# Projections in feature-major form with 512 tokens a matmul, and block-diagonal rotary queries for the sample, in a two-layer streaming encoder

## The chip, the cores and the metric

The kernel runs on one core of one Trainium2 chip. The metric is the device time of one execution in microseconds (us). A measurement of this kernel's time is good to some tenths of a per cent.

## The reference

Two layers of an encoder run over two groups of inputs with the same weights: a prompt of 1,024 tokens (one sequence) and a sample of 8 sequences of 16 tokens each, which continue caches of 512 earlier frames. Width is 1,024. In each layer one projection of x gives everything else:

```python
h = jnp.einsum('btd,de->bte', x, w_in)
(c_q, c_kv, k_rope, g_mla, f_q, f_k, f_v, f_logit, g_fox, m_q, g_mem) = jnp.split(h, split_idx, axis=-1)
```

Three kinds of attention follow, four heads each. MLA: queries and keys from low-rank latents (`c_q` of 384, `c_kv` of 256), with a part of 128 and a rotary part of 64 per head; a query sees keys up to its chunk of 64. Forgetting attention ("fox"): heads of 64, causal, with a bias of summed log forget values. Memory attention: heads of 64 over 256 memory rows. Each output is multiplied by `silu` of its gate (`g_mla`, `g_fox`, `g_mem`), all go through `w_out`, and `y = LayerNorm(alpha * x + out)`. For the sample the MLA score of a query against a cached frame is the product of latents (256) plus the product of rotary parts (64). Outputs are both y and the new cache rows. Everything is float32.

## The kernel before

**Precision.** Most matmuls take split operands: a value is a high part (`fp32r`) plus a low part, and `mm3` (L189) adds three products per pair: high by high, high by low, low by high (lines L193 to L195 of the profile). `split` (L173) makes the parts: a copy on ACT, a subtraction on DVE. `wsplit` (L183) does it for weights, with the subtraction on DVE or POOL. The sample's attention uses plain float32 operands (`mm`, L197).

**x^T.** A layer's input lies transposed in SBUF: feature on the partition, token along the row. Before, `X` has four entries, one per 256 tokens, each of two halves of four feature chunks (tiles of 128 x 4 x 256, high and low); a fifth entry is the sample. `xtok` (L253) cuts 128 tokens of one chunk out of it. In the first layer `xload` in `main` (L1462) loads x^T ready-made from DRAM in pieces of 512 KB and splits it; in the second `xpair` (L224) transposes two finished output tiles on TensorE and splits them. The first two pairs are made in the tail of the first layer, the last two are read back from DRAM after it (`after0`, L1494).

**Two forms of projection.** `tokproj` (L284) has tokens on the output's partitions: 128 tokens of x^T are the stationary operand, the weights move (up to 306 columns). `featproj` (L287) is feature-major: 128 weight columns are stationary, one entry of x^T moves, 256 tokens, into half a PSUM bank; 8 chunks x 3 products = 24 matmuls a group. It is used by `gates` (L356: memory gate `ge`, fox gate `gf`, two MLA gates `gm0`, `gm1`, each 2 x 4 groups and one token-major group for the sample) and by `qproj` (L343: memory queries, 2 x 4 groups, and fox queries, 4 groups for each half of the heads). Groups go to one of two `psx` banks or, while `self.bg` is set, of three `pss` banks that attention scores use too.

**Order of the work** (`layer`, L1293): memory gate, with `mem_prep` (keys and values of the prompt's memory) put in after `GE0` steps of it in the first layer; memory queries; memory attention with the first half of the fox keys and the fox gate as filler; for each half p of the fox heads: keys and values, queries, then `foxu`, eight units of two heads by four blocks, with one step of MLA gate p and one of the sample's work as filler before each; low-rank projections; MLA; `w_out` and LayerNorm as the tail. `gates` is a generator: one `yield` is one step of filler. A unit's second half (transposes, product with the values) runs one unit later. This is the order in which instructions are given; the order on each engine's queue is fixed at build by a scheduler that takes an instruction as soon as it is ready on a simulated timeline (`schedule_with_timeline_sim=True`, L1628), those given earlier first.

**Slots.** Tiles share pools: `u` 25 slots of 4 KB per partition (x^T takes 16 and 2 for the sample), `w` 8 for weights, `pw` 5 (among others the raw pieces of x^T, of the memory input, and softmax rows). A new tile waits for a free slot.

**Sample rotary queries.** `s_qrope` (L826) projects and rotates the queries of 128 sample tokens, transposes them, and stores them with 64 partitions to DRAM (`qd[2]`, third part). `s_q` (L961) loads them for a pair of sequences in three DMAs: latents, the rotary part on partitions 0 to 63, and once more the second sequence's columns on partitions 64 to 127. `s_scores` (L989) then takes the rotary product of sequence b on partitions 64b to 64b+63 alone; the cached rotary keys (`kr`) lie with one sequence on each half of the partitions. `s_scores_new` (L1001) multiplies by the new keys (`krt`, 64 partitions).

Of the kernel before, what the change touches and what calls it, by code (L numbers as in the profile page):

```python
# [10 lines left out]
F32R = mybir.dt.float32r  # L11
# [40 lines left out]
GE0 = 4  # L52
# [29 lines left out]
class Enc:  # L82
# [141 lines left out]
    def xpair(self, tiles, banks=None):  # L224

        out = []
        for kh in range(2):
            hi = self.u([P, 4, 256], F32R, "xh")
            lo = self.u([P, 4, 256], F32R, "xl")
            for kk in range(2):  # L230
                ps = (banks or [self.pst])[kk % len(banks or "1")]()
                v = ps.rearrange("p (k t) -> p k t", k=2)
                for a in range(2):
                    for b in range(2):
                        k = kh * 4 + kk * 2 + a
                        self.tr(v[:, a, b * P:(b + 1) * P], tiles[b][:, k * P:(k + 1) * P])
                self.split(hi[:, kk * 2:kk * 2 + 2, :], lo[:, kk * 2:kk * 2 + 2, :], v)
            out.append((hi, lo))
        return out
# [13 lines left out]
    def xtok(self, X, i, k):  # L253

        if i == 8:
            return tuple(t[:, k, :] for t in X[4])
        return tuple(t[:, k % 4, (i % 2) * P:(i % 2 + 1) * P] for t in X[i // 2][k // 4])
# [29 lines left out]
    def featproj(self, ps, X, j, W, f):  # L287
        self.mm3(ps, [(tuple(t[:, f * P:(f + 1) * P] for t in W[k]),
                       tuple(t[:, k % 4, :] for t in X[j][k // 4])) for k in range(8)])
# [53 lines left out]
    def qproj(self, X, W, f, q, scale):  # L343

        nc = self.nc
        for j in range(4):
            ps = self.psj()
            self.featproj(ps, X, j, W, f)
            c = slice(j * 256, (j + 1) * 256)
            for e in range(2):  # L350
                a, b = slice(e * 64, e * 64 + 64), slice(64 - e * 64, 128 - e * 64)
                nc.scalar.activation(q[e][a, c], ps[a, :], AF.Copy, scale=scale)
                nc.vector.scalar_tensor_tensor(q[e][b, c], ps[a, :], scale, self.f(q[e][a, c]), op0=ALU.mult, op1=ALU.subtract)


    def gates(self, l, X, src, chunks, more=None, raws=None):  # L356
# [3 lines left out]
        for j in range(4):  # L360
            if more is not None:
                next(more)
            if j == 3:
# [6 lines left out]
            for f in range(2):  # L370
                ps = self.psj()
                self.featproj(ps, X, j, W, f)
                g = self.st([P, 256], name="gg")
                nc.scalar.activation(g, ps, AF.Tanh, scale=0.5)
                nc.vector.scalar_tensor_tensor(g, g, 1.0, ps, op0=ALU.add, op1=ALU.mult)
                self.store(self.gd[chunks[f]][:, j * 256:(j + 1) * 256], g)
                if j == 3 and f == GTF:
# [297 lines left out]
    def lowrank(self, l, X, more):  # L675
# [7 lines left out]
        self.krt = H[4][0:64, 0, RQ:512]  # L683
# [60 lines left out]
        def turn8():  # L744
# [5 lines left out]
            nc.scalar.copy(self.krt, turn(krs, (8,))[0:64, 0:P])  # L750
# [75 lines left out]
    def s_qrope(self, l, dst):  # L826
# [11 lines left out]
        Q = self.pw([64, 4, 2, 64], name="qrs")  # L838
        for h in range(4):
            e, g = h % 2, h // 2  # L840
            self.qput(Q, h, pt[e * 64:e * 64 + 64, g * P:(g + 1) * P], MLA_SCALE)
        self.store(dst[0:64], Q.rearrange("p a b r -> p a (b r)"))
# [118 lines left out]
    def s_q(self, kind, n, p):  # L961

        t = self.sp.tile([P, 3, P], F32, tag="qv", bufs=QV_BUFS, name=self.nm("qv"))
        self.load(t[:, :2], self.qd[kind][:, :2, p])
        if n == 3:
            self.load(t[0:64, 2], self.qd[kind][0:64, 2, p])
            self.load(t[64:128, 2, 64:128], self.qd[kind][0:64, 2, p, 64:128])
        return t
# [20 lines left out]
    def s_scores(self, ps, q, K, kr):  # L989

        for a in range(len(K[0])):
            cols = slice(a * 256, (a + 1) * 256)
            for c in range(3):
                for b in range(2):
                    r = slice(b * 64, b * 64 + 64)
                    if c < 2:
                        self.mm(ps[r, cols], q[:, c, r], K[b][a][:, c, :], c == 0, False)
                    else:
                        self.mm(ps[r, cols], q[r, 2, r], kr[r, cols], False, True)

    def s_scores_new(self, o, q, new, kr):  # L1001

        for c in range(2):
            self.mm(o, q[:, c, :], new[:, c * P:(c + 1) * P], c == 0, False)
        self.mm(o, q[0:64, 2, :], kr, False, True)
# [449 lines left out]
    def main(self):  # L1455
# [6 lines left out]
        def xload(j):  # L1462
            out = []
            for kh in range(2):
                t = self.pw([P, 4, 256], name="x")
                self.load(t, i["x_t"][j, kh])
                if j == 0:
                    raws.extend(self.wload(i["w_ge"][0][kh:kh + 1]))
                hi = self.u([P, 4, 256], F32R, "xh")
                lo = self.u([P, 4, 256], F32R, "xl")  # L1470
                for c in (slice(0, 2), slice(2, 4)):
                    self.split(hi[:, c], lo[:, c], t[:, c])
                out.append((hi, lo))
            X.append(out)

        def more():
            for j in range(1, 4):
                xload(j)
                if j == 2:
                    self.late_consts()  # L1480
                yield
# [5 lines left out]
            X.append((hi, lo))  # L1487
            yield
# [5 lines left out]
        def after0(t, y):  # L1494
            self.store(yd[t], y)
            hold.append(y)
            if t == 8:
                xs1 = self.xsample(hold.pop())
                for j in range(NXD, 4):
# [5 lines left out]
                    nx.append(self.xpair(tl, [self.pst, self.pss]))  # L1505
# [3 lines left out]
            elif len(hold) == 2:  # L1509
                nx.append(self.xpair(list(hold)))  # L1510
# [19 lines left out]
def packed(i):  # L1530
# [27 lines left out]
    d["x_t"] = i["x_prompt"].reshape(4, 256, 2, 4, P).transpose(0, 2, 4, 3, 1)  # L1558
# [73 lines left out]
```

## Time and profile before

| | |
|---|---|
| median of 3 runs | 1437.47 us (1436.8 to 1440.21) |
| profiled execution, own time | 1439.67 us |
| its span, first to last instruction | 1437.9 us |
| mean granted clock of TensorE | 0.994 |
| busy: DVE, ACT, POOL | 53%, 43%, 36% of the span |
| data moved | 180.64 MB, 126 GB/s on average |

The profile is one execution on the chip. A row of a group gives line, engine, operation, output<-inputs (of a matmul: moving, then stationary operand), the piece of the array, the shape, the count, then busy time in us, mean duration of one in ns, and the idle time before it with what ended it. PE is TensorE's matmul, PEld its weight load, DVE VectorE, ACT ScalarE, POOL GpSimd, SP the engine that issues the DMAs. Matmuls are pipelined, so their durations overlap; a timeline row gives the start, then the duration. In the chain of waits the work that ended last is followed back from the end.

### The profile page before, as it was taken

The page shows a single profiled execution, that of the slowest core. Times are in us where ns is not written, and L with a number is a line of the kernel's source. Part 1 is how long each engine was busy: PE and PEld are TensorE (multiplying, and loading weights), DVE is VectorE, ACT ScalarE, POOL GpSimd, SP SyncE. Part 2 cuts the span into 40 slices and gives each one's busy share as a digit, 9 for nine tenths or more (in the row PEclk, how much of TensorE's full clock was granted, in tenths as well). Part 3 has the DMA queues.
Part 4 walks back from the last instruction along what each step waited for, and adds up shares of the span by engine and source line. Part 5 has one row for each costly group of instructions (what it writes and reads, how often), then busy time and mean ns, then how long its engine had stood idle before and what let it go on. Part 6 is the DMA issues. An engine that isn't in the chain of part 4 may idle for free.

```text
span 1437.9 us, 27746 instructions
## 1 busy us (share of the span) xinstructions
PE 1402.4 (98%) x10222; PEld 1257.8 (87%) x10222; DVE 756.6 (53%) x1863; ACT 620.8 (43%) x1624; POOL 515.8 (36%) x722
## 2 busy tenths in 40 slices
PE   7999999999999999999999999999999999999997
PEld 6999989989988788888899999899899887887885
DVE  6236555266045665666663365643642565566664
ACT  6344454354255544722233454544533554455100
POOL 0233254354364221712322234434625541235121
PEclk9999999999999999999999999999999999999999
DMA  7223332345254431363541234234443633234531
GB/s 286 91 73 91 113 126 87 124 140 166 83 176 130 133 115 53 132 215 118 181 160 54 85 101 153 78 89 137 142 148 113 203 95 123 96 114 143 165 118 73
DMA packets 142344, 180.64 MB, mean 126 GB/s; under 512 B 32384, under 2 KB 99776, under 8 KB 142208
## 3 DMA queue, kind: packets, MB, share of 16 engines
q1 hardware_dynamic: 142208, 178.86, 38.6%
q8 instruction: 81, 1.33, 0.4%
q14 instruction: 55, 0.45, 0.1%
HBM read 138.69 MB, written 40.12 MB: 124 GB/s over the span
## 4 chain that ended last, share of the span: by engine, by line
PE 87%; DMA 4%; DVE 3%; ACT 2%; POOL 2%; issue 1%; SPq 0%; POOLq 0%; DVEq 0%; ACTq 0%
PE pss L193 15%; PE pss L195 14%; PE pss L194 14%; PE pss L198 10%; PE pso L198 7%; PE pst L202 7%; PE psx L198 6%; PE psx L193 4%; PE psx L195 4%; PE psx L194 4%; DMA memx<-in_mem_t_dram 1%; POOL wl L187 1%; PE psx L202 1%; DMA raw<-in_w_uqn_dram 1%; DMA g<-md 1%
## 5 line engine op out<-in xcount | busy, mean ns | idle before, releaser
L187 POOL TENSOR_TENSOR wl<-raw,wh 128x1024 fp32r<-128x1024 f32 (+3 forms) x40 | 101.6, 2543 | 208.1 <-ACT wh L184 98.1
L178 DVE TENSOR_TENSOR ptw<-pst,ptw 128x512 fp32r<-128x512 f32 (+1 forms) x192 | 122.0, 642 | 55.2 <-ACT ptw L177 53.8
L177 ACT CAST ptw<-pst 128x512 fp32r<-128x512 f32 (+1 forms) x192 | 103.4, 552 | 97.3 <-PE pst L202 88.9
L193 PE MATMUL pss<-wh,xh 128*128 128x306 f32 (+1 forms) x384 | 118.2, 309 | 0.4 <-ACT h L693 0.4
L195 PE MATMUL pss<-wh,xl 128*128 128x306 f32 (+1 forms) x384 | 117.6, 307 | 0.0
L194 PE MATMUL pss<-wl,xh 128*128 128x306 f32 (+1 forms) x384 | 117.5, 307 | 0.0
L193 PE MATMUL psx<-xh,wh 128*128 128x256 f32 x384 | 109.9, 287 | 7.8 <-ACT wh L184 6.7
L193 PE MATMUL pss<-woh,msh 128*128 128x512 f32 x288 | 114.0, 396 | 0.7 <-ACT msh L1251 0.6
L195 PE MATMUL pss<-woh,msl 128*128 128x512 f32 x288 | 114.0, 397 | 0.1
L194 PE MATMUL pss<-wol,msh 128*128 128x512 f32 x288 | 113.6, 394 | 0.0
L193 PE MATMUL pss<-xh,wh 128*128 128x256 f32 x384 | 109.9, 286 | 0.2
L194 PE MATMUL psx<-xl,wh 128*128 128x256 f32 x384 | 109.8, 286 | 0.0
L195 PE MATMUL psx<-xh,wl 128*128 128x256 f32 x384 | 108.9, 285 | 0.0
L195 PE MATMUL pss<-xh,wl 128*128 128x256 f32 x384 | 108.4, 282 | 0.0
L194 PE MATMUL pss<-xl,wh 128*128 128x256 f32 x384 | 108.3, 282 | 0.0
L396 POOL TENSOR_SCALAR pa<-pa,col 128x128 f32<-128x128 f32 (+3 forms) x64 | 47.7, 750 | 109.4 <-DVE col L395 62.0
L193 PEld LDWEIGHTS psx<-xh,wh 128*128 128x128 f32 x384 | 73.6, 192 | 8.5 <-ACT wh L184 6.7
L198 PE MATMUL pso<-ptw,vh 128*128 128x256 f32 (+1 forms) x336 | 73.7, 296 | 2.3 <-DVE ptw L178 1.3
L193 PEld LDWEIGHTS pss<-xh,wh 128*128 128x128 f32 x384 | 72.5, 189 | 2.9 <-DVE col L431 1.5
L184 ACT CAST wh<-raw 128x1024 fp32r<-128x1024 f32 (+4 forms) x52 | 54.8, 1057 | 45.7 <-PE pss L194 14.4
L193 PEld LDWEIGHTS pss<-wh,xh 128*128 128x128 f32 x384 | 72.4, 189 | 2.2 <-ACT h L693 1.8
L195 PEld LDWEIGHTS pss<-wh,xl 128*128 128x128 f32 x384 | 72.3, 189 | 1.6 <-issue 1.6
(364 smaller groups left out, 4198.9 us busy)
## 6 DMA issues: line engine op xcount, KB each, us to landing
gd<-gg SPq DMA_DIRECT2D x64, 128.0 KB
kT<-in_fox_kt_dram SPq DMA_DIRECT2D x32, 256.0 KB
vraw<-in_fox_v_dram SPq DMA_DIRECT2D x32, 256.0 KB
kT<-in_mla_kt_dram SPq DMA_DIRECT2D x32, 256.0 KB
vraw<-in_mla_v_dram SPq DMA_DIRECT2D x32, 256.0 KB
raw<-in_w_out_dram SPq DMA_DIRECT2D x16, 512.0 KB
g<-md SPq DMA_DIRECT2D x16, 512.0 KB
raw<-in_w_lr_dram SPq DMA_DIRECT2D x8, 612.0 KB
```

The source lines that it names most:

```text
L177: nc.scalar.copy(hi, ps)
L178: nc.vector.tensor_tensor(lo, ps, self.f(hi), op=ALU.subtract)
L184: self.nc.scalar.copy(hi, raw)
L187: (self.nc.vector if dve else self.nc.gpsimd).tensor_tensor(lo, raw, self.f(hi), op=ALU.subtract)
L193: self.nc.tensor.matmul(ps, ah, bh, start=first and x == 0, stop=False)
L194: self.nc.tensor.matmul(ps, ah, bl, start=False, stop=False)
L195: self.nc.tensor.matmul(ps, al, bh, start=False, stop=last and x == n - 1)
L198: self.nc.tensor.matmul(ps, lhsT, rhs, start=start, stop=stop)
L202: self.nc.tensor.transpose(out, in_, self.ident[:k, :k])
L396: self.nc.gpsimd.tensor_scalar(p, p, rs, 1.0, op0=ALU.mult, op1=ALU.mult)
```

## The change

x^T is held as two entries of 512 tokens, each of four quarters of two feature chunks (tiles of 128 x 2 x 512); pool slots in all are as many as before. `xhalf` allocates an entry, and `xpair` fills the columns of its 256 tokens. `featproj` moves 512 tokens into a full bank, and `gates` and `qproj` loop over two entries. A gate is evicted in two halves of 256 columns; its generator has 5 steps where it had 9. In the first layer `xload` loads quarters of 512 KB, and the sample's x is loaded in the same step as the second entry; `GE0` becomes 2. The sample's rotary queries are written block-diagonally, with zeros, on 128 partitions, loaded in one DMA, and multiplied over the full 128 partitions; `krt` keeps the copy of the keys that the transpose gives on partitions 64 to 127.

```diff
-GE0 = 4
+GE0 = 2
...
+    def xhalf(self):
+
+        return [(self.u([P, 2, 512], F32R, "xh"), self.u([P, 2, 512], F32R, "xl")) for _ in range(4)]
+
+    def xpair(self, X, j, tiles, banks=None):
+
+        if j % 2 == 0:
+            X.append(self.xhalf())
+        c = slice(j % 2 * 256, j % 2 * 256 + 256)
+        for kk, (hi, lo) in enumerate(X[j // 2]):
+            ps = (banks or [self.pst])[kk % len(banks or "1")]()
+            v = ps.rearrange("p (k t) -> p k t", k=2)
+            for a in range(2):
+                for b in range(2):
+                    k = kk * 2 + a
+                    self.tr(v[:, a, b * P:(b + 1) * P], tiles[b][:, k * P:(k + 1) * P])
+            self.split(hi[:, :, c], lo[:, :, c], v)
...
     def featproj(self, ps, X, j, W, f):
         self.mm3(ps, [(tuple(t[:, f * P:(f + 1) * P] for t in W[k]),
-                       tuple(t[:, k % 4, :] for t in X[j][k // 4])) for k in range(8)])
+                       tuple(t[:, k % 2, :] for t in X[j][k // 2])) for k in range(8)])
...
     def qproj(self, X, W, f, q, scale):
-        for j in range(4):
-            ps = self.psj()
+        for j in range(2):
+            ps = self.psw()
             self.featproj(ps, X, j, W, f)
-            c = slice(j * 256, (j + 1) * 256)
+            c = slice(j * 512, (j + 1) * 512)
...
     def gates(self, l, X, src, chunks, more=None, raws=None):
-        for j in range(4):
+        for j in range(2):
             if more is not None:
                 next(more)
-            if j == 3:
+            if j == 1:
...
             for f in range(2):
-                ps = self.psj()
+                ps = self.psw()
                 self.featproj(ps, X, j, W, f)
-                g = self.st([P, 256], name="gg")
-                nc.scalar.activation(g, ps, AF.Tanh, scale=0.5)
-                nc.vector.scalar_tensor_tensor(g, g, 1.0, ps, op0=ALU.add, op1=ALU.mult)
-                self.store(self.gd[chunks[f]][:, j * 256:(j + 1) * 256], g)
+                for q in range(2):
+                    g = self.st([P, 256], name="gg")
+                    s = ps[:, q * 256:q * 256 + 256]
+                    nc.scalar.activation(g, s, AF.Tanh, scale=0.5)
+                    nc.vector.scalar_tensor_tensor(g, g, 1.0, s, op0=ALU.add, op1=ALU.mult)
+                    self.store(self.gd[chunks[f]][:, j * 512 + q * 256:j * 512 + q * 256 + 256], g)
...
-        self.krt = H[4][0:64, 0, RQ:512]
+        self.krt = H[4][:, 0, RQ:512]
...
     def s_qrope(self, l, dst):
-        Q = self.pw([64, 4, 2, 64], name="qrs")
+        Q = self.pw([P, 4, 2, 64], name="qrs")
+        self.nc.gpsimd.memset(Q, 0.0)
         for h in range(4):
             e, g = h % 2, h // 2
-            self.qput(Q, h, pt[e * 64:e * 64 + 64, g * P:(g + 1) * P], MLA_SCALE)
-        self.store(dst[0:64], Q.rearrange("p a b r -> p a (b r)"))
+            src = pt[e * 64:e * 64 + 64, g * P:(g + 1) * P].rearrange("p (a b t) -> p a b t", b=2, t=TS)
+            for b in range(2):
+                self.nc.scalar.activation(Q[b * 64:b * 64 + 64, :, b, h * TS:(h + 1) * TS], src[:, :, b, :], AF.Copy, scale=MLA_SCALE)
+        self.store(dst, Q.rearrange("p a b r -> p a (b r)"))
...
     def s_q(self, kind, n, p):
-        self.load(t[:, :2], self.qd[kind][:, :2, p])
-        if n == 3:
-            self.load(t[0:64, 2], self.qd[kind][0:64, 2, p])
-            self.load(t[64:128, 2, 64:128], self.qd[kind][0:64, 2, p, 64:128])
+        self.load(t[:, :n], self.qd[kind][:, :n, p])
...
     def s_scores(self, ps, q, K, kr):
-                    if c < 2:
-                        self.mm(ps[r, cols], q[:, c, r], K[b][a][:, c, :], c == 0, False)
-                    else:
-                        self.mm(ps[r, cols], q[r, 2, r], kr[r, cols], False, True)
+                    self.mm(ps[r, cols], q[:, c, r], K[b][a][:, c, :] if c < 2 else kr[:, cols], c == 0, c == 2)
...
     def s_scores_new(self, o, q, new, kr):
-        for c in range(2):
-            self.mm(o, q[:, c, :], new[:, c * P:(c + 1) * P], c == 0, False)
-        self.mm(o, q[0:64, 2, :], kr, False, True)
+        for c in range(3):
+            self.mm(o, q[:, c, :], new[:, c * P:(c + 1) * P] if c < 2 else kr, c == 0, c == 2)
...
         def xload(j):
+            X.append(self.xhalf())
+            for kk, (hi, lo) in enumerate(X[j]):
+                t = self.pw([P, 2, 512], name="x")
+                self.load(t, i["x_t"][j, kk])
+                if j == 0 and kk % 2 == 0:
+                    raws.extend(self.wload(i["w_ge"][0][kk // 2:kk // 2 + 1]))
+                for c in range(2):
                     self.split(hi[:, c], lo[:, c], t[:, c])
...
         def more():
+            xload(1)
             t = self.pw([P, 8, P], name="x")
             self.load(t, i["xs_t"])
             hi = self.u([P, 8, P], F32R, "xsh")
             lo = self.u([P, 8, P], F32R, "xsl")
             self.split(hi, lo, t)
             X.append((hi, lo))
+            self.late_consts()
+            yield
             yield
```

More of the change, by code (lines that the diff above doesn't have):

```diff
@@ L221, in late_consts @@
         self.load(self.sin, self.i["k_sin"])
[L224 to L239, printed above, removed]
+    def xhalf(self):
[12 more added lines that the diff above has]
+            self.split(hi[:, :, c], lo[:, :, c], v)
     def xsample(self, t):
@@ L255, in xtok @@
         if i == 8:
-            return tuple(t[:, k, :] for t in X[4])
-        return tuple(t[:, k % 4, (i % 2) * P:(i % 2 + 1) * P] for t in X[i // 2][k // 4])
+            return tuple(t[:, k, :] for t in X[2])
+        return tuple(t[:, k % 2, (i % 4) * P:(i % 4 + 1) * P] for t in X[i // 4][k // 2])
     def wload(self, src, alloc=None):
@@ L370, in gates @@
             for f in range(2):
-                ps = self.psj()
+                ps = self.psw()
                 self.featproj(ps, X, j, W, f)
-                g = self.st([P, 256], name="gg")
-                nc.scalar.activation(g, ps, AF.Tanh, scale=0.5)
-                nc.vector.scalar_tensor_tensor(g, g, 1.0, ps, op0=ALU.add, op1=ALU.mult)
-                self.store(self.gd[chunks[f]][:, j * 256:(j + 1) * 256], g)
-                if j == 3 and f == GTF:
+                for q in range(2):
[4 more added lines that the diff above has]
+                    self.store(self.gd[chunks[f]][:, j * 512 + q * 256:j * 512 + q * 256 + 256], g)
+                if j == 1 and f == GTF:
                     pt = self.pst()
@@ L749, in turn8 @@
                 nc.scalar.copy(self.sx[:, 1, c * P:(c + 1) * P], pt[:, 0:P])
-            nc.scalar.copy(self.krt, turn(krs, (8,))[0:64, 0:P])
+            nc.scalar.copy(self.krt, turn(krs, (8,))[:, 0:P])
             self.store(o["s_lat"][l].rearrange("b t r -> (b t) r"), sl)
@@ L1462, in xload @@
         def xload(j):
[L1463 to L1471, printed above, removed]
+            X.append(self.xhalf())
[5 more added lines that the diff above has]
+                for c in range(2):
                     self.split(hi[:, c], lo[:, c], t[:, c])
-                out.append((hi, lo))
-            X.append(out)
         def more():
[L1477 to L1481, printed above, removed]
+            xload(1)
             t = self.pw([P, 8, P], name="x")
@@ L1504, in after0 @@
                         tl.append(t)
-                    nx.append(self.xpair(tl, [self.pst, self.pss]))
+                    self.xpair(nx, j, tl, [self.pst, self.pss])
                 nx.append(xs1)
@@ L1509, in after0 @@
             elif len(hold) == 2:
-                nx.append(self.xpair(list(hold)))
+                self.xpair(nx, t // 2, list(hold))
                 hold.clear()
@@ L1557, in packed @@
     d["w_ukv_v"] = ukv[..., P:].reshape(L, 2, P, 2, 2, P).transpose(0, 3, 2, 1, 4, 5)
-    d["x_t"] = i["x_prompt"].reshape(4, 256, 2, 4, P).transpose(0, 2, 4, 3, 1)
+    d["x_t"] = i["x_prompt"].reshape(2, 512, 4, 2, P).transpose(0, 2, 4, 3, 1)
     d["xs_t"] = i["x_sample"].reshape(P, 8, P).transpose(2, 1, 0)
```

## The prediction

> **What bounds the kernel now.** I read the page first: the busy line, then the chain that ended last.
>
> ```profile
> span 1437.9 us, 27746 instructions
> PE 1402.4 (98%) x10222; PEld 1257.8 (87%) x10222; DVE 756.6 (53%) x1863; ACT 620.8 (43%) x1624; POOL 515.8 (36%) x722
> PE 87%; DMA 4%; DVE 3%; ACT 2%; POOL 2%; issue 1%; SPq 0%; POOLq 0%; DVEq 0%; ACTq 0%
> PE psx L193 <- ACT wh L184: 7.3, 2, 6.7
> ```
>
> TensorE bounds it: 98% busy, 87% of the chain, and in the view of its waits (last line) the longest is 6.7 us, the wait for the first data. So a gain must shorten the stream of matmuls or close one of the few holes. The groups of instructions by line and shape show what the change touches: the six rows with x as the moving and w as the stationary operand.
>
> ```profile
> L193 PE MATMUL psx<-xh,wh 128*128 128x256 f32 x384 | 109.9, 287 | 7.8 <-ACT wh L184 6.7 <-DVE qm L353 0.6 <-DVE gg L375 0.3
> L194 PE MATMUL psx<-xl,wh 128*128 128x256 f32 x384 | 109.8, 286 | 0.0
> L195 PE MATMUL psx<-xh,wl 128*128 128x256 f32 x384 | 108.9, 285 | 0.0
> L193 PE MATMUL pss<-xh,wh 128*128 128x256 f32 x384 | 109.9, 286 | 0.2
> L195 PE MATMUL pss<-xh,wl 128*128 128x256 f32 x384 | 108.4, 282 | 0.0
> L194 PE MATMUL pss<-xl,wh 128*128 128x256 f32 x384 | 108.3, 282 | 0.0
> ```
>
> 6 x 384 = 2,304 matmuls of 256 columns become 1,152 of 512. The trap is the mean of 285 ns: it is the time from start to end of one pipelined matmul, not what each adds. What counts is the step from start to start, read from the timeline where one kind runs unbroken. The fence has first and last row of three runs: 57 matmuls of 256 columns (a projection), then 51 and 56 of 512 (the output projection).
>
> ```profile
> 174.99 0.28 PE L193 MATMUL pss<-xh,wh 128*128 128x256 f32 x1
> 181.58 0.28 PE L195 MATMUL pss<-xh,wl 128*128 128x256 f32 x1
> ...
> 628.58 0.39 PE L193 MATMUL pss<-woh,msh 128*128 128x512 f32 x1
> 640.14 0.39 PE L195 MATMUL pss<-woh,msl 128*128 128x512 f32 x1
> ...
> 705.32 0.48 PE L194 MATMUL pss<-wol,msh 128*128 128x512 f32 x1
> 718.12 0.39 PE L195 MATMUL pss<-woh,msl 128*128 128x512 f32 x1
> ```
>
> 6.59 us over 56 steps is 117.7 ns; 11.56 over 50 is 231.2; 12.80 over 55 is 232.7. Two narrow steps, 235.4 ns, are hardly longer than one wide one: the step grows almost with the columns.
>
> **The change, part by part.** *Wide projections.* A pair saves 235.4 - 232.7 = 2.7 to 235.4 - 231.2 = 4.2 ns, times 1,152: 3.1 to 4.8 us. I take 4.0. The weight loads that go away are 1,152 of 10,222, but they bring no more than this, because the wide rows already have one load per 512 columns. The evictions of the gates keep their shapes and counts; those of the queries move the same elements in half as many instructions. DVE and ACT, at 53% and 43%, gain what nobody waits for. A projection group holds its bank for 24 x 232 ns = 5.6 us where it was 2.8, but there are half as many.
>
> *Rotary queries of the sample.* The timeline around one score block of the sample attention:
>
> ```profile
> 461.90 0.61 PE L198 MATMUL psx<-sx,qv 128*128 128x128 f32 x4
> 462.44 0.48 PE L198 MATMUL psx<-h,qv 64*128 64x128 f32 x2
> 462.86 0.65 PE L198 MATMUL psx<-kT,qv 128*64 128x256 f32 x2
> ...
> 465.86 0.65 PE L198 MATMUL psx<-krs,qv 64*64 64x256 f32 x4
> 466.44 1.08 PE L198 MATMUL psx<-kT,qv 128*64 128x256 f32 x6
> 466.92 0.59 PE L198 MATMUL psx<-kT,qv 128*64 128x256 f32 x2
> ```
>
> The third column of such a row is the piece of the array (rows*columns). The four rotary instructions on 64*64 pieces take 465.86 to 466.44 = 0.58 us until another kind follows. Four on 128*64 pieces, followed by their own kind, take 466.44 to 466.92 = 0.48. With the zeros in place the rotary part has the shape of its neighbours, so the changes of shape into it and out of it go, about 0.1 us each. There are 16 such groups (2 layers, 4 pairs, 2 key halves): up to 3.2 us. For the new keys, two instructions on 64*128 take 0.42 us after four on 128*128 that take 0.54, or 0.27 a pair: 0.15 us, 8 times, 1.2 us. Since the neighbours aren't always adjacent in the order (466.44 is a six, not a four), the bounds are 0 and 4.4; I take 3.0, nearer the rows than zero. By the Trainium skill, page "TensorEngine Tiling (Array Packing)", section Theoretical Speedup, a contraction of 64 should rather be packed, for up to twice the speed, which speaks against padding it to 128; by that the 16 groups would cost up to 16 x 0.58 = 9.3 us more. The same page, Key Properties, says that switching the tiling mode drains the engine, which speaks for it. The rows side with the second: four instructions take no less time in the 64*64 form.
>
> *Its other work.* The query's block gets a memset on POOL, eight small ACT instructions for four, and a store twice as large, while each later load is one DMA where it was three.
>
> ```profile
> 439.61 0.50 SPq L168 DMA_DIRECT2D qd<-qrs  x1
> L847 ACT ACTIVATE qrs<-pso x8: 270/272/275, 438.5 to 1149.1; 64x128 f32<-64x128 f32 x8
> ```
>
> Four more instructions of at most 0.27 us delay that store on SP's queue by 1.1 us, and the weight loads queued behind it as well. The first use is at 462.44, so over 20 us cover it: nothing. Without the cover, 1.1 us twice.
>
> *Start.* x^T came in eight loads with the memory keys' input queued after six; now all eight and the sample's x go first, three loads of 512 KB more.
>
> ```profile
> x<-in_x_t_dram SPq DMA_DIRECT2D x8, 512.0 KB
> 0.00:21.00 21.00, 14.01 (x96) 13.78 (x96) 13.91 (x21) 13.42 (x22) 0.43 (x6) 1.00 0.86 321
> 21.00:41.00 20.00, 16.21 (x104) 14.94 (x103) 10.45 (x17) 10.21 (x19) 0.01 (x1) 0.83 0.56 205
> 13.41 8.47 DMA memx<-in_mem_t_dram
> 22.57 0.39 PE L193 MATMUL psx<-wh,mxh 128*128 128x256 f32 x1 [1.39 <-ACT mxh L177]
> ```
>
> In the two window rows the figures after the length are busy times of PE, PEld, DVE, ACT and POOL, then clock, DMA share and GB/s. The first 21 us run at 321 GB/s, so 1.57 MB more ahead is 4.9 us. Before, TensorE already waits for this input (last row) and then sits idle 20.0 - 16.2 = 3.8 us between 21 and 41 at a clock of 0.83, worth 0.17 x 20 = 3.4 us more: a hole of about 7. Against the delay stands that the second half of x, 11.1 us of ready projections (48 x 232 ns), now arrives before the memory keys and can run in the hole, if the order on TensorE's queue lets it. Bounds: +4.9 and -7.2. I take 0.
>
> *Fill.* The gates run as filler between attention units. A gate has five steps instead of nine, so with one per unit the eight units of a forget-attention stage are filled only up to the fifth.
>
> ```profile
> 288.00:350.00 62.00, 60.77 (x549) 54.85 (x549) 40.64 (x121) 33.98 (x83) 36.10 (x51) 1.00 0.46 135
> 237.32 2.82 POOL L187 TENSOR_TENSOR wl<-raw,wh 128x1208 fp32r<-128x1208 f32 x1 [0.18 <-PE pss L194]
> 238.62 0.30 PE L193 MATMUL pss<-wh,xh 128*128 128x302 f32 x1
> 244.44 0.60 PE L202 MATMUL pst<-ident,pf 128*128 128x128 f32 x4
> ```
>
> A stage (first row) has 60.8 us of TensorE, of which the gate's nine groups are 9 x 24 x 117.7 ns = 25.4. The last three units hold 3,200 of 9,216 score columns, 35%: without gate they are 0.35 x 35.4 = 12.4 us for TensorE and 0.35 x 40.6 = 14.2 for DVE. So 1.8 us short per stage, 7 us for the four stages, if nothing else fills. But the other rows show that something else does: the matmuls on 302 columns, which belong to the next stage, already run at 238.62 between the transposes of this stage's scores (244.44). They start when the gate's last matmul frees a slot for their split weights (POOL's row, released by PE). An earlier end of the gate frees that slot earlier. I take 2 us; bounds 0 and the rival's price below.
>
> *Layer boundary.* The second layer's first half of x is complete in the tail of the first; its 11.1 us of projections, as long as four narrow groups before, cover the transposes of the second half.
>
> ```profile
> PE pss L202 <- DMA x<-yd: 0.4, 1, 0.4
> ```
>
> The one wait there is 0.4 us. Bounds 0 to 2 (one pair's four splits); I take 0.
>
> **Sum.** The profiled execution took 1439.7 us, 1.8 around its span and 2.2 above the median of 1437.5. 1439.7 - 4.0 - 3.0 + 0 + 2 = 1434.7, in the median's terms 1432.5. That is -0.35%; a measurement tells about 0.3%, 4.3 us, from no change.
>
> **The rivals.** A is the forecast: 1428 to 1436 by the bounds of the first two parts and some of the others. B: the hole at the start closes; 1432.5 - 7.2 = 1425. For it: the data are there; against: the order is fixed at build, and before it left the hole with projections waiting. C: the memory keys come late and the order keeps them first: 1432.5 + 4.9 = 1437, no change; the row at 22.57 speaks for it. D, the slower side: the last three units of the forget attention stand bare. Their chain per unit is at least a reduction, an exponential and a normalisation:
>
> ```profile
> L431 DVE CUSTOM_DVE_ANT_0 pf<-pss,pf 128x512 f32<-128x512 f32 x10 | 6.8, 685 | 4.9 <-PE pss L198 4.8
> L433 ACT ACTIVATE pf<-pf,col 128x896 f32<-128x896 f32 x2 | 2.1, 1041 | 0.0
> L396 POOL TENSOR_SCALAR pf<-pf,col 128x896 f32<-128x896 f32 x2 | 2.0, 1018 | 4.7 <-DVE col L395 4.7
> ```
>
> Together 2.7 us; half of it bare in 12 units (3 in each of 4 stages) is 16 us: 1432.5 - 2 + 16 = 1447. It decides from 11 us on, 0.9 per unit. E: the wide step costs twice the narrow one and the shapes gain nothing: 1437. F, the other way: that weight loads set the pace. Two windows, of narrow and of wide matmuls:
>
> ```profile
> 175.00:181.50 6.50, 6.50 (x58) 6.50 (x57) 2.53 (x6) 1.88 (x5) 2.17 (x3) 1.00 0.87 270
> 657.20:664.20 7.00, 7.00 (x32) 5.69 (x32) 3.97 (x6) 2.02 (x3) 0.00 (x0) 1.00 0.63 225
> ```
>
> PEld is busy all of the first and 81% of the second. If each load were worth a step, 1,152 x 117.7 ns = 136 us would go: 1302. The step of 231 ns rules it out; no chance is left for it. The Trainium skill, "Perfetto Trace Analysis", section Identifying the Most-Contended Engine, judges TensorE's headroom by just this busy share; here the step decides.
>
> **How the numbers follow.** A 0.52, B 0.12, C 0.17, D 0.12, E 0.07. A's range is cut by the bound of 0.3% at 1433.2; its parts with little lost fill lie below it, so of A 0.38 counts as faster and 0.14 as no change. Faster 0.38 + 0.12 = 0.50; same 0.14 + 0.17 + 0.07 = 0.38; slower 0.12. The range 1422 to 1444 holds A, B, C and E and the lower part of D. A's own is 1428 to 1436.
>
> **What would show it.** In the profile after: 1,152 matmuls of 128x512 with x moving, stepping by 231 to 233 ns; rotary scores on 128*64 pieces; PE still about 98%. Wrong would be: new waits of TensorE on col or ptw between 200 and 350 (D), a later first matmul on mxh with idle time before it (C), a fuller window from 21 to 41 (B), or a wide step of 235 and more (E).

## The result, and the profile after

The changed kernel takes 1460.37 us (median of 4 runs, 1459.48 to 1461.69), the kernel before 1437.93 beside it (4 runs): a ratio of 1.0152, 95% interval 1.0135 to 1.0168. It is 22 us slower, where 5 us faster was forecast and the range ended at 1444.

The page of the changed kernel: span, busy line, chain.

```profile
span 1458.2 us, 25367 instructions
PE 1407.4 (97%) x9070; PEld 1207.9 (83%) x9070; DVE 748.0 (51%) x1831; ACT 615.4 (42%) x1600; POOL 515.6 (35%) x724
PE 46%; DVE 1%; ACT 1%; DMA 1%; POOL 1%; issue 1%; POOLq 0%; DVEq 0%; SPq 0%; ACTq 0%
```

There are 1,152 matmuls fewer, and TensorE is idle 1458.2 - 1407.4 = 50.8 us where it was 35.5. The other 5 us by which the span grew are busy time, in spite of the fewer matmuls; the mean granted clock is 0.987 where it was 0.994. The shares of the chain add to half of the span, so it was followed back only so far and says little here. The waits of TensorE (total, times, longest):

```profile
PE psx L193 <- ACT wh L184: 6.7, 1, 6.7
PE pso L198 <- ACT ptw L177: 5.7, 6, 2.4
PE psx L193 <- ACT mxh L177: 4.9, 1, 4.9
PE psx L202 <- POOL spr L399: 4.1, 2, 2.0
PE pss L198 <- DVE col L434: 3.8, 5, 1.5
```

Three of these rows in the kernel before:

```profile
PE pso L198 <- ACT ptw L177: 2.2, 6, 0.6
PE psx L193 <- ACT mxh L177: 1.4, 1, 1.4
PE pss L198 <- DVE col L431: 1.0, 2, 0.5
```

The waits that the prediction named as its refutation are there. The one on mxh is C's. The one of 2.4 us on ptw lies between 200 and 350 us, where D put it. Those on col come to 0.6 us in that stretch; the longest, 1.5 us, ends at 186.5, at the start of the forget attention. The 4.1 us on spr, the sample's softmax rows, no rival had. Two rows of the timeline, 17 steps apart, say that the wide step is as forecast: 3.95 us / 17 = 232.4 ns.

```profile
226.19 0.40 PE L193 MATMUL pss<-xh,wh 128*128 128x512 f32 x1
230.14 0.39 PE L195 MATMUL pss<-xh,wl 128*128 128x512 f32 x1
```

So the time is lost elsewhere. Windows in the first layer's forget attention, of the kernel before and then of the changed one (length; busy PE, PEld, DVE, ACT, POOL; clock; DMA share, GB/s), with the changed kernel's start in the last two rows:

```profile
178.00:190.00 12.00, 12.00 (x100) 10.94 (x100) 4.50 (x16) 6.71 (x15) 9.89 (x14) 1.00 0.70 230
218.00:242.00 24.00, 23.90 (x195) 22.81 (x194) 13.19 (x39) 12.24 (x28) 11.59 (x17) 1.00 0.21 65
330.00:352.00 22.00, 22.00 (x211) 20.65 (x209) 15.45 (x36) 9.82 (x26) 11.84 (x16) 1.00 0.49 145
```

```profile
178.00:190.00 12.00, 7.76 (x48) 5.06 (x48) 6.74 (x16) 4.67 (x13) 8.52 (x11) 0.83 0.76 241
218.00:242.00 24.00, 22.72 (x143) 17.68 (x141) 14.22 (x44) 12.24 (x30) 16.19 (x20) 1.00 0.37 110
330.00:352.00 22.00, 19.40 (x115) 15.04 (x115) 13.61 (x42) 10.70 (x24) 18.46 (x25) 0.87 0.65 209
0.00:21.00 21.00, 13.76 (x48) 10.70 (x48) 12.60 (x19) 13.54 (x23) 0.43 (x6) 1.00 0.85 324
21.00:41.00 20.00, 15.51 (x117) 15.22 (x118) 11.67 (x20) 11.10 (x20) 1.67 (x3) 0.91 0.62 227
```

Three places lose TensorE: the start of the forget attention, and the end of each of its halves. The second layer repeats them. The start of the kernel looks as it did.

### The profile page after: what moved, and what is told of

Read it like the earlier page. It is cut to its first block, busy times and chain, and to the rows that moved or that the text cites. A ratio compares the mean times of both kernels' runs of the same rounds, so it can differ in the third digit from the quotient of the medians.

```text
span 1458.2 us, 25367 instructions
## 1 busy us (share of the span) xinstructions
PE 1407.4 (97%) x9070; PEld 1207.9 (83%) x9070; DVE 748.0 (51%) x1831; ACT 615.4 (42%) x1600; POOL 515.6 (35%) x724
## 4 chain that ended last, share of the span: by engine, by line
PE 46%; DVE 1%; ACT 1%; DMA 1%; POOL 1%; issue 1%; POOLq 0%; DVEq 0%; SPq 0%; ACTq 0%
PE pss L193 8%; PE pss L195 8%; PE pss L194 8%; PE pss L198 5%; PE pso L198 4%; PE pst L202 3%; PE psx L198 3%; PE psx L194 2%; PE psx L193 2%; PE psx L195 2%; PE psx L202 1%; DMA g<-md 0%; DVE ptw L178 0%; DMA raw<-in_w_uqn_dram 0%; POOL wl L187 0%
## 5 line engine op out<-in xcount | busy, mean ns | idle before, releaser
L193 PE MATMUL psx<-xh,wh 128*128 128x512 f32 x192 | 76.8, 402 | 6.7 <-ACT wh L184 6.7
L193 PE MATMUL pss<-xh,wh 128*128 128x512 f32 x192 | 79.0, 412 | 0.0
L194 PE MATMUL pss<-xl,wh 128*128 128x512 f32 x192 | 77.3, 403 | 0.0
L195 PE MATMUL pss<-xh,wl 128*128 128x512 f32 x192 | 76.9, 401 | 0.0
L194 PE MATMUL psx<-xl,wh 128*128 128x512 f32 x192 | 76.7, 401 | 0.0
L195 PE MATMUL psx<-xh,wl 128*128 128x512 f32 x192 | 76.0, 399 | 0.0
L194 PEld LDWEIGHTS pss<-wl,xh 128*128 128x128 f32 x384 | 72.8, 190 | 0.0
L587 POOL TENSOR_SCALAR pf<-ckb,ncq 128x640 f32<-128x640 f32 (+3 forms) x64 | 47.3, 751 | 69.5 <-PE pst L202 53.9
```

The lines of the kernel that those rows point to most:

```text
L193: self.nc.tensor.matmul(ps, ah, bh, start=first and x == 0, stop=False)
L194: self.nc.tensor.matmul(ps, ah, bl, start=False, stop=False)
L195: self.nc.tensor.matmul(ps, al, bh, start=False, stop=last and x == n - 1)
L587: nc.gpsimd.tensor_scalar(p[:, :n], ckb[:, :n], 1.0, ncq[:, h, i:i + 1], op0=ALU.mult, op1=ALU.add)
```

## The experiments

Eighteen kernels, each timed against the kernel before on its own chip, so ratios are compared. 0.1% is 1.44 us.

### Portions

**Fine portions.** The changed kernel, every wide group of a gate given in two portions of four chunks, so that a gate has nine again.

```diff
-                self.featproj(ps, X, j, W, f)
+                self.featproj(ps, X, j, W, f, range(4))
+                yield
+                self.featproj(ps, X, j, W, f, range(4, 8))
...
-GE0 = 2
+GE0 = 4
```

> The kernel after, but each wide gate group is given in two steps of four chunks, so that a gate has nine steps again. Theory S (steps): the loss comes from a gate that is given in five large portions, which leaves later attention units without filler; then nearly all of the 22 us comes back, plus the saving of the wide matmuls: 1430 to 1438 us. Theory B (bank): the loss comes from a wide group that holds one of the three score banks twice as long; here it holds it across two units, longer still: 1455 to 1470 us.

Measured: 1442.53 us, 1.0023 (1.0010 to 1.0035). That is between the two ranges, nearer to the first. 1.29% of the time is back, 18.6 us. The kernel is still slower than before, though, and the wait for the sample's keys, 1.3 us in the changed kernel and none in the kernel before, has grown:

```profile
PE psx L198 <- DMA kT<-in_mem_kt_dram: 7.4, 2, 3.8
```

**Coarse portions alone.** The kernel before, narrow matmuls, the forget and MLA gates in the five portions of the change.

```diff
-        for j in range(4):
+        for jj in range(2):
...
             for f in range(2):
+                for j in (2 * jj, 2 * jj + 1):
                     ps = self.psj()
                     self.featproj(ps, X, j, W, f)
```

> The kernel before, all matmuls narrow, but the fox gate and the two MLA gates are given in five steps in the order of the kernel after (two narrow groups a step). S: the loss of the kernel after comes without any wide matmul, 1455 to 1466 us. B: a bank is held as briefly as before, so no change, 1435 to 1440 us.

Measured: 1457.03 us, 1.0123 (1.0097 to 1.0149), without one wide matmul. Its window at the end of the first half stands at 20.17 of 24 us busy, where the kernel before has 23.90:

```profile
218.00:242.00 24.00, 20.17 (x171) 18.05 (x170) 14.88 (x49) 12.78 (x30) 14.82 (x19) 0.99 0.32 98
```

**MLA gates only**, from both sides: the changed kernel with these gates narrow in nine portions (gates_n is the old loop on the new tiles), and the kernel before with these alone in five.

```diff
-            gm = self.gates(l, X, f"w_gm{p}", (2 * p, 2 * p + 1))
+            gm = self.gates_n(l, X, f"w_gm{p}", (2 * p, 2 * p + 1))
```

> The kernel after, but the two MLA gates, which fill the forget attention, move 256 tokens a matmul in nine steps as before; all other projections stay wide. S and B both take the loss in the forget attention away, except for what the fox gate's five steps and the wide fox queries do to its start (idle time at 180 to 188 us in the profile after, the same in layer 1: about 6 us and a slow clock after it, each time): 1432 to 1438 if the start depends on the MLA gate, 1445 to 1450 if it does not.

```diff
-            gm = self.gates(l, X, f"w_gm{p}", (2 * p, 2 * p + 1))
+            gm = self.gates_c(l, X, f"w_gm{p}", (2 * p, 2 * p + 1))
```

> The kernel before, with the MLA gates alone in five portions (narrow matmuls, order and portions of the change); the forget gates stay in nine. With both in five the time was 1457.0, 17.2 us over the kernel before. Theory Portions, sized by the profile of that run: the forget attention with what follows to the first up-projection took 5.7 us a layer longer and the memory attention 2.3: here 1450 to 1453. Rival: most of the loss is what the memory units leave undone when the forget attention begins: under 1446.

Measured: 1449.11 us, 1.0062 (1.0039 to 1.0085), and 1449.03, 1.0066 (1.0046 to 1.0085), which is just under its range. On the changed kernel 0.90%, 13.0 us, is back; the stall at the start of the forget attention stays (7.25 of 12 us busy from 178 to 190). On the kernel before coarse MLA gates cost 0.66%, 9.5 us; by difference, the other 0.57% of the coarse portions is the forget gates', among the memory units, a place that no rival of the prediction held.

### The change without wide matmuls

**Rotary alone**, on the kernel before: the change's s_qrope, s_q, s_scores, s_scores_new and krt.

```diff
-        self.krt = H[4][0:64, 0, RQ:512]
+        self.krt = H[4][:, 0, RQ:512]
...
-                        self.mm(ps[r, cols], q[r, 2, r], kr[r, cols], False, True)
+                    self.mm(ps[r, cols], q[:, c, r], K[b][a][:, c, :] if c < 2 else kr[:, cols], c == 0, c == 2)
```

> The kernel before with the block-diagonal rotary queries alone. The prediction's term: 3 us less (bounds 0 and 4.4), 1433 to 1437 us; no theory of the loss expects a loss here. If it loses, the rotary part has a share in the 22 us.

Measured: 1434.49 us, 0.9964 (0.9953 to 0.9976).

**All narrow.** The changed kernel with 256 columns a matmul everywhere; x in quarters, the loads' order and the rotary stay.

```diff
-            ps = self.psw()
-            self.featproj(ps, X, j, W, f)
-            c = slice(j * 512, (j + 1) * 512)
+            ps = self.psj()
+            self.narrow(ps, X, j, W, f)
+            c = slice(j * 256, (j + 1) * 256)
```

> The changed kernel with every projection narrow again (256 columns a matmul, gates in nine portions, queries in four groups): x^T in quarters, the loads' order of the start and the block-diagonal rotary queries stay. Beside it stands the rotary alone, 1434.5 us. Theory Start: the memory keys, queued behind all of x, cost what PE waits for them at 20 us (5.1 us in the changed kernel against 1.55 before): 1437 to 1440. Rival: the rest of x is there earlier for it, as the memory part ended at 39.4 us in the changed kernel against 41.2 before, so layout and order are worth nothing: 1433 to 1436, and all that the version in fine portions (1442.5) lost against the rotary alone comes from the wide groups themselves.

Measured: 1434.85 us, 0.9971 (0.9958 to 0.9983), the same as the rotary alone. The rival holds: layout and order of loads are worth nothing in sum. Wide groups in fine portions (1.0023) then cost 0.52%, though their steps are shorter.

### Start and queries

**Late x**: fine portions, the second half of x after the memory's loads. **Narrow queries**: fine portions, the forget queries in four groups. **All three repairs.** **Late x, all narrow.**

```diff
         def more():
+            yield
             xload(1)
...
             self.late_consts()
             yield
-            yield
```

> The changed kernel in half-group portions (1442.5 us), and the second half of x, the sample's x and the tables loaded only after the memory's loads, before the second two gate groups. Theory Start: the wait for the memory keys at 21 us falls from 5.25 us to under 2 us and the time to 1437 to 1440. Rival: the second half of x is then late by as much, so that the gate groups after the memory part wait for it: 1441 to 1445, with a wait on x between 35 and 50 us.

```diff
-            self.qproj(X, W, 0, QF, -S64)
+            self.qproj(X, W, 0, QF, -S64, False)
```

> The changed kernel in half-group portions (1442.5 us) with the forget queries alone projected narrow, four groups of 256 columns in place of two of 512. Theory Banks: two wide query groups hold two of the three score banks while the forget sums' transposition, the last memory units and the first forget scores queue behind, so the stall at the start of each forget attention (3.9 and 3.8 us at 181 and 895 us, with the wait on the sample's keys) comes from them: gone here, 1434 to 1438. Rival: the stall comes from the order in which gates, sample and memory units were left by then, and stays: the kernel loses only the gain of the wide query steps (4 groups of 24 matmuls, about 0.1 us each): 1442 to 1445.

The third has both edits:

> The changed kernel with the three repairs together: gate groups in half-group portions, the second half of x after the memory's loads, the forget queries narrow. Alone on top of the fine portions the second gave 0.45% and the third 0.39%. If they lie in different places (20 to 45 us; 175 to 190 us), they add: 1429 to 1433, no wait over 2 us between 20 and 40 or between 175 and 190 us. Rival: they lean on the same wait for the sample's keys, since what starts earlier finds them later: 1435 to 1438.

The fourth is the all-narrow kernel with the edit of more():

> The changed kernel with every projection narrow (1434.9 us with its own order of loads) and the second half of x after the memory's loads. Theory Start: the gain of that order is no matter of wide groups; the first 40 us lose 10 us to waits in the narrow version and 4.7 in the wide one with that order: 1429 to 1431. Rival: the narrow version's gate groups come to the memory part later or earlier, so that the order does nothing for it: 1434 to 1436. Beside the run with the three repairs it also says what the wide groups are worth when nothing else is in their way.

Measured, the first a little under its range: 1436.63 us, 0.9978 (0.9968 to 0.9989); 1437.91, 0.9984 (0.9972 to 0.9996); 1435.55, 0.9970 (0.9959 to 0.9982); 1429.96, 0.9930 (0.9916 to 0.9943). The order of loads is worth 0.45% with wide groups and 0.41% with narrow ones. The window of the start shows it in the first of them, 18.72 of 20 us at full clock; neither the kernel before (16.2 at 0.83) nor the changed one has that:

```profile
21.00:41.00 20.00, 18.72 (x142) 17.45 (x142) 12.47 (x21) 12.75 (x23) 2.41 (x4) 1.00 0.65 234
```

The two repairs do not add: 0.9970 where the sum was 0.9939. The rival had the time right but not the reason, since the wait on the sample's keys was down to 2.7 us. With all three repairs the wide kernel is still 0.4% behind the narrow one.

### Score banks

**MLA gates in the other ring**: the three repairs, and the gates' groups take one of the sample's two banks. **MLA gates narrow**, in score banks. **All narrow, gates in the other ring.**

```diff
-                ps = self.psw()
+                ps = self.psx()
                 self.featproj(ps, X, j, W, f, range(4))
```

> As the run with the three repairs, and the MLA gates' wide groups, which lie among the forget units, take one of the two banks of the other ring, that the sample uses, in place of one of the three score banks. Theory Banks: wide groups cost their gain because each keeps a score bank for twice as long, so the units' scores wait: at least 3 us faster than the run with the three repairs. Rival: the score banks are no limit once the portions are fine; then the time is the same within 2 us, or longer by up to 5 us where the sample's steps wait for their banks instead.

```diff
-            gm = self.gates(l, X, f"w_gm{p}", (2 * p, 2 * p + 1))
+            gm = self.gates_n(l, X, f"w_gm{p}", (2 * p, 2 * p + 1))
```

> As the run with the three repairs, and the MLA gates narrow in nine portions, so that only the other gates and the memory queries are wide. Theory Steps: the wide groups there are worth their shorter steps, 384 matmuls by 2 x 117.7 - 232 = 3.4 ns, 1.3 us: slower by 1 to 2 us, at the edge of what the rounds can tell. Theory Banks: narrow groups there are better, 2 to 5 us faster.

```diff
-                ps = self.psj()
+                ps = self.psx()[:, 0:256]
                 self.narrow(ps, X, j, W, f)
```

> All projections narrow, x's second half after the memory's loads (1430.0 us), with the gates' narrow groups in the sample's banks in place of the score banks. Theory Banks in its strict form: a narrow group leaves its score bank in time, so this does nothing: 1428 to 1432, and the wide gates in those banks (1426.0) are then worth 2 to 6 us more than narrow ones. Rival: any gate group in a score bank holds the units up: 1421 to 1426, and wide groups are worth nothing even here.

Measured: 1425.95 us, 0.9906 (0.9892 to 0.9920); 1428.31, 0.9921 (0.9907 to 0.9934); 1430.20, 0.9930 (0.9916 to 0.9945). Wide groups in score banks 0.9970, wide elsewhere 0.9906, narrow in score banks 0.9921; where all is narrow the bank changes nothing (0.9930 both times). In fine portions it is the wide group in a score bank that costs, 0.5 to 0.6%; the gain with narrow MLA gates, 7 us, was more than either theory expected.

### Portions or banks

**The changed kernel, coarse, gates in the other ring**, and **the coarse kernel before, likewise**:

```diff
-                ps = self.psw()
+                ps = self.psx()
                 self.featproj(ps, X, j, W, f)
```

> The changed kernel as it is, five coarse portions and its own start, with one edit: the gates' wide groups take a bank of the ring of two that the sample uses, in place of one of the three score banks. Theory Portions: the last units of each forget attention have no gate left to cover them, whatever bank the gates take; of the loss only what the bank gave the fine version (0.64%) comes back: 1449 to 1454. Theory Banks: the loss of the coarse portions is the score bank held for two portions' worth: 1434 to 1440.

```diff
-                    ps = self.psj()
+                    ps = self.psx()[:, 0:256]
                     self.featproj(ps, X, j, W, f)
```

> The kernel before with the gates in five coarse portions of narrow matmuls (1457.0 us with score banks), the gates now in the sample's banks. Theory Portions: 1450 to 1457. Theory Banks: 1438 to 1445. In between: both have a share, to be read beside the changed kernel with the same edit.

**Spread**: the changed kernel, and the one with the gates in the other ring, with the five MLA portions at units 1, 3, 5, 7 and 8.

```diff
+            def spread(g):
+                for x, _ in enumerate(g):
+                    yield
+                    if x < 3:
+                        yield
+
-            gm = self.gates(l, X, f"w_gm{p}", (2 * p, 2 * p + 1))
+            gm = spread(self.gates(l, X, f"w_gm{p}", (2 * p, 2 * p + 1)))
```

> The changed kernel with one edit: the MLA gates' five coarse portions are given at units 1, 3, 5, 7 and 8 of each half of the forget attention in place of units 1 to 5. Theory Bare end: the loss is what the last three units wait for when no gate is left: the 0.66% that coarse MLA gates cost on the kernel before comes back, 1449 to 1454. Theory Long pieces: a portion of 24 wide matmuls (5.6 us) lies too long between two units, and a unit without one is bare wherever it lies: 1457 to 1464.

> The same spreading on the changed kernel whose gates take the sample's banks (1457.2 us). Theory Bare end: the waits between 220 and 240 us (8.4 us over the bare steps there) go and 1443 to 1449 is reached. Theory Long pieces: 1454 to 1460, with the waits spread over the half in place of its end.

Measured: 1457.17 us, 1.0112 (1.0097 to 1.0127); 1449.74, 1.0067 (1.0050 to 1.0084); 1455.00, 1.0107 (1.0086 to 1.0128); 1444.65, 1.0045 (1.0028 to 1.0063). The first three lie outside the ranges of their theories, the last within that of the bare end. The bank gives back 0.40% on the changed kernel and 0.56% on the coarse kernel before. Spreading the changed kernel gives 0.45%, and 0.67% where the gates are in the other ring. Both exist. On the coarse kernel before every group is narrow: two of them in one portion in score banks cost as well, and of the 0.66% of its MLA gates the other ring leaves 0.10%, less than the noise of the two runs. The windows of the changed kernel with only the bank changed, then of the one with the bank changed and the portions spread, part the two:

```profile
178.00:190.00 12.00, 12.00 (x62) 10.01 (x61) 4.59 (x12) 4.82 (x10) 6.95 (x6) 1.00 0.42 129
218.00:242.00 24.00, 19.42 (x123) 14.92 (x123) 15.71 (x44) 13.03 (x32) 14.22 (x21) 0.79 0.29 84
```

```profile
218.00:242.00 24.00, 23.45 (x168) 20.35 (x167) 17.64 (x49) 14.32 (x34) 17.53 (x22) 1.00 0.37 111
330.00:352.00 22.00, 21.89 (x173) 20.18 (x172) 16.21 (x41) 12.32 (x32) 14.28 (x18) 1.00 0.58 172
```

The other ring fills the stall at 178 to 190 (12.00 of 12, from 7.76) and leaves the bare end worse (19.42 of 24 at a clock of 0.79, from 22.72 at 1.00); spreading fills the end. Spread without the other ring, the kernel keeps the stall (7.55 of 12).

**The version that follows**: fine portions, late x, gates and all queries wide in the other ring.

```diff
-                ps = self.psw()
+                ps = self.psx()
                 self.featproj(ps, X, j, W, f, range(4))
...
-            ps = self.psw()
+            ps = self.psx()
             self.featproj(ps, X, j, W, f)
             c = slice(j * 512, (j + 1) * 512)
```

> The run with the gates in the sample's banks (1426.0 us: fine portions, late second half of x, forget queries narrow), with the forget queries wide again, they too in the sample's banks. Theory Banks: the stall of 3.7 us at the start of each forget attention came from the two score banks that the wide queries held; it stays away and their shorter steps are a gain of 0.5 to 1 us: 1423 to 1427. Rival: it came from the order (the units' and the sample's work queued behind long groups): 1430 to 1434, with the wait on the sample's keys at 175 and 885 us back.

Measured: 1423.12 us (4 runs), 0.9879 (0.9865 to 0.9894): 17.6 us faster than the kernel before. The kernel with all narrow and the gates in the other ring (0.9930) is 0.51%, 7.3 us, behind, but its forget queries lie in score banks, so this holds their move to the other ring as well. With those queries narrow in score banks on both sides (0.9906 and 0.9930), wide groups are worth 0.24%, 3.5 us, good to about 3 us.

```profile
178.00:190.00 12.00, 11.70 (x54) 7.78 (x54) 5.66 (x18) 4.50 (x10) 7.29 (x12) 1.00 0.64 207
218.00:242.00 24.00, 23.91 (x177) 21.59 (x176) 11.01 (x32) 12.14 (x29) 11.89 (x15) 1.00 0.37 104
```

## Why the prediction was wrong

The ladder: before 1, rotary 0.9964, with layout and order 0.9971, with wide groups in fine portions 1.0023, with coarse portions 1.0152. The steps are -5.2, +1.0, +7.5 and +18.6 us, where the prediction's sum had -3, 0, -4 and +2.

**Fill is the step that failed**: "I take 2 us", because "something else does" fill. Coarse portions cost 17.7 us on the kernel before (1.0123), 8 of them by the banks (0.56%) and, by difference, 8 by the forget gates' portions (0.57%). The term counted the forget attention alone and so put the forget gates, among the memory units, at nothing; the banks it did not have. In the forget attention the reading of two rows was at fault. That the next stage's matmuls on 302 columns start when the gate frees a slot for their weights is half of their condition. In the kernel before, the last scores of the half had gone out by then, and the gate itself ran on behind them, to 238.50:

```profile
230.88 0.28 PE L198 MATMUL pss<-fkl,qf 128*128 128x256 f32 x1
```

In the changed kernel the weights are indeed split earlier, at 229.45 for 237.32, and the gate ends at 232.0. The units' scores go on to 238.50, and only behind them, at 242.06, later than before, does the next stage begin:

```profile
229.45 2.81 POOL L187 TENSOR_TENSOR wl<-raw,wh 128x1208 fp32r<-128x1208 f32 x1
232.00 0.40 PE L195 MATMUL pss<-xh,wl 128*128 128x512 f32 x1
238.50 0.28 PE L198 MATMUL pss<-fkl,qf 128*128 128x256 f32 x1
242.06 0.41 PE L193 MATMUL pss<-wh,xh 128*128 128x302 f32 x1 [0.21 <-DVE col L434]
```

The changed kernel with the gates in the other ring shows it most plainly: the split is done at 217.6, and the matmuls that it is for start 22.5 us later.

```profile
214.82 2.80 POOL L187 TENSOR_TENSOR wl<-raw,wh 128x1208 fp32r<-128x1208 f32 x1 [0.90 <-PE psx L194]
219.54 0.39 PE L195 MATMUL psx<-xh,wl 128*128 128x512 f32 x1
234.12 0.28 PE L198 MATMUL pss<-fkl,qf 128*128 128x256 f32 x1
240.16 0.39 PE L193 MATMUL pss<-wh,xh 128*128 128x302 f32 x1
```

In all twenty traces (first layer, first half) they start 2.7 to 8.9 us after the last scores of that half, never ahead of them, whether the gate ends before or after. They take score banks behind the units; whether the bank or the order of TensorE's queue holds them wasn't tried. Rival D, with 16 us and a chance of 0.12, had the place of the MLA gates and about their size (9.5 us on the kernel before, 13.0 on the changed one), but took the bare chain alone for the cause, without the banks, and lacked what the forget gates lose. Of the changed kernel's distance to the last version, what coarse portions cost even when spread was not parted further.

**Wide projections**: the step was right, but one sentence under it was wrong: "A projection group holds its bank for 24 x 232 ns = 5.6 us where it was 2.8, but there are half as many." Half as many didn't make up for it. At the start of the forget attention POOL's bias waits for the forget sums' rows, loaded at 180.7 where it was 175.0, while the scores came earlier (178.5 for 184.3). Issues of that load, before and after:

```profile
L165 SPq DMA_DIRECT2D ckb<-ckd x2: 342/380/417, 175.0 to 177.3; - x2
```

```profile
L165 SPq DMA_DIRECT2D ckb<-ckd x2: 511/547/583, 180.7 to 187.1; - x2
```

All three score banks are then held by scores that can't be reduced, and the gate that could cover this needs one of them. In the other ring it covers it. The waits of TensorE between 170 and 200 us, and the row of the bias:

```profile
PE psx L202 <- POOL spr L399: 2.0, 1, 2.0
PE pss L198 <- DVE col L434: 1.5, 1, 1.5
PE psx L198 <- DMA kT<-in_mem_kt_dram: 0.7, 1, 0.7
184.93 4.35 POOL L587 TENSOR_SCALAR pf<-ckb,ncq 128x640 f32<-128x640 f32 x5 [0.41 <-DMA ckb<-ckd]
```

So only part of the idle time ends with a score bank; the rest ends with work of the sample that stands in the queue ahead of the gate. The bias starts 6.4 us after the first scores (178.5) in the changed kernel and 5.9 us after them with fine portions, but 0.2 us with the forget queries narrow as well, and 1.0 us in the last version, where they are wide in the other ring. The late sums thus come from wide queries in score banks; through which wait is not shown. The term itself, 4.0 us, is borne out as far as the runs can tell: 960 of the 1,152 matmuls measured 3.5 us, where the forecast saving gives 3.3.

**Rotary**: right in kind, 5.2 us (3.5 to 6.8) for 3.0. In the profile of that run, counted from each start to the next matmul's, the scores on the old keys take 27.5 us where they took 30.7, those on the new keys 4.9 where they took 7.3. The forecast had 3.2 at most for the first and 1.2 for the second. At the old keys the gain lies with the neighbours, as forecast: the 128 steps on kT fell from 167 to 136 ns each, while the 64 rotary steps went from 145 to 157. The rotary scores run on 128*64 pieces:

```profile
469.93 0.65 PE L198 MATMUL psx<-krs,qv 128*64 128x256 f32 x4
470.51 0.38 PE L193 MATMUL pss<-wv,lth 128*128 128x256 f32 x1
```

Four take 0.58 us here, as four on 64*64 did, so padding costs next to nothing. Packing was not tried.

**Start**: 0 was right as a sum, of two opposite parts: the first matmul on the memory's input comes at 25.42 for 22.57, after a wait of 4.9 us for 1.4, but the last comes at 39.29 for 41.07, as three waits between 30 and 34 us, 2.1 us in all, are gone. That the gate groups which came forward fill them was not tried apart. Of the lower bound, 7.2 us, another order of loads got 4.9 (0.9964 to 0.9930). **Layer boundary**: none of the changed kernel's five waits above lies there, as said. **Its other work**, taken at nothing, shows one wait of 0.5 us, for the sample's queries in the first layer (waits of the changed kernel between 455 and 480 us; the kernel before has none of it):

```profile
PE psx L198 <- DMA qv<-qd: 0.5, 1, 0.5
```

## What to carry to other kernels

Count a filler in portions and ask for each unit, above all the last ones, which portion covers it and which bank that portion needs; portions twice as long cover half as many units. Work that is "next" fills a hole only if neither its bank nor its place in the queue lies behind the work that stalls: look for the last instruction of the stalled stage, not for the wait that ended last. Widening a matmul pays by its step only where its longer hold on a bank is nobody's wait.

## What the runs showed of the hardware

A stall costs more than its length. After the gaps at 178 to 190 us of the changed kernel, 0.7, 2.0 and 1.5 us, seven steps of a wide group took 2.99 us, 427 ns each, where they take 232 at full clock:

```profile
188.84 0.63 PE L194 MATMUL pss<-xl,wh 128*128 128x512 f32 x1
191.83 0.63 PE L195 MATMUL pss<-xh,wl 128*128 128x512 f32 x1
```

The Trainium skill, "TensorE: Matmul & The Clock Gate", section Wait — 56ns, not 53.3ns?, gives 426.7 ns for 512 columns on the cold array: the trace agrees. Its advice in Why this matters for your kernels, no idle gaps over about 3 us, was not enough here: with shorter gaps close together, 4.2 us idle in 12, the clock of that window was 0.83, where the changed kernel with the gates in the other ring, busy throughout, had 1.00.
